# Both out projections of a two-layer encoder trunk by Strassen's algorithm on 12 of 16 K tiles

## The chip, the cores and the metric

The kernel runs on one core of a Trainium2 chip. The metric is device time in microseconds (us) of the whole program. A core has TensorE (PE in the profile: matmuls; PEld: the load of the stationary operand, here called the weight load), VectorE (DVE), ScalarE (ACT), GpSimd (POOL), and SyncE (SP), whose queue issues most transfers. Each engine works through its own queue in order; semaphores join them.

## The reference

The trunk has two layers over 512 tokens of width 2048, in float32. The change touches the last product of each layer, `concat([...]) @ w_out`, with a residual added:

```python
def even_layer(x, ...):
    proj = rmsnorm(x, ln_g) @ w_in
    ...
    return x + jnp.concatenate([na_o, dn_o, mem_o], axis=-1) @ w_out   # (512, 2048) @ (2048, 2048)

def odd_layer(x, ...):
    ...
    return x + jnp.concatenate([diff_o, mem_o], axis=-1) @ w_out       # (512, 2048) @ (2048, 2048)
```

Each branch (`na_o`, `dn_o`, `mem_o`, `diff_o`) is multiplied by its SiLU gate before the concatenation.

## The kernel before, in words

Activations lie transposed: 16 K tiles of 128 features (partitions) by 512 tokens. A float32 product is made as three matmuls on operands that are split into a high and a low part: high weight by high activation, high by low, low by high. ACT makes the high part (a rounding copy), DVE the low part (a subtraction). Tiles named `wr` are raw weights from DRAM, `wh` and `wl` their high and low parts, `hi` and `lo` those of activations, `w` (or `w2`) general work tiles of 128 by 512, `pa` the PSUM banks.

`WStream` holds all weights in the order of their use. Each time that PE's code takes a unit of weights, the stream emits the splits for the unit that is three ahead (`SPLIT_BUFS = 3` buffers each of `wh` and `wl`) and loads for raw tiles beyond that. PE's order is that in which the code is written. The orders on DVE, ACT, POOL and SP are made by a scheduler at build time and are fixed in the program: an instruction that waits holds up everything behind it on its engine.

`gates` ends a layer: for each of 16 tiles a product of 48 matmuls (`group`: 16 K tiles times 3, weights stationary, 512 token columns moving), then a SiLU on DVE and ACT, and a multiplication into the tile `mix[i]`. `out_proj` follows: for each of 16 output tiles `j` one `group` over the 16 K tiles, whose operands `mh[k]`, `ml[k]` are split from `mix[k]` by the hook `make` during the first. `consume` adds the residual, which comes by a transfer on SP's queue: `to_x1` (layer 0) also stores the sum to DRAM (`x1_d`), adds its squares to `acc1` and splits it into the operands `xh`, `xl` of layer 1; `to_out` (layer 1) stores the output. Gate weights and out-projection weights come in raw tiles of 128 by 1024 (eight K tiles of 128 columns). Long-lived operands have a pool of 34 tiles (`hl`, 17 pairs), work tiles another of 34 (`NW2`). Layer 0's branch outputs wait for their gates in DRAM (`mix_d`, `keep`); layer 1's stay in SBUF.

## Time and profile before

| what | value |
|---|---|
| median of 3 runs (lowest to highest) | 2024.88 us (2024.31 to 2026.25) |
| profiled execution, span from first to last instruction | 2021.8 us |
| PE busy | 2002.1 us, 99% of the span |
| DVE, ACT, POOL busy | 1155.9, 759.7, 129.8 us |
| mean granted TensorE clock | 0.998 of full speed |
| HBM traffic | 106 GB/s over the span |

No other time of the profiled execution is given than its span; the median of the runs is 3.1 us above it. Busy shares are means over stages. Where PE is busy throughout a stage, only its own instructions count there. A matmul's recorded duration covers its passage through the array, and the next one starts before it ends: what a matmul costs is read from the distance between two starts.

### The profile page before, as it was taken

What the parts mean: (1) busy time and instruction counts of PE and PEld (TensorE: products, weight loads), DVE (VectorE), ACT (ScalarE), POOL (GpSimd) and SP (SyncE); (2) the same over time, 40 slices, a digit from 0 to 9 for tenths busy, and PEclk for the clock granted to TensorE, in tenths of its full rate; (3) what the DMA queues carried; (4) which work ended last, traced back from release to release, by engine and by line L of the source; (5) the groups of instructions that cost most, each with busy time, mean ns of one, the idle gap of its engine ahead of it and who ended that gap; (6) DMA issues with size and microseconds to landing.
All of it is one profiled execution on the core that took longest, in us unless ns stands there. A gap on an engine that the chain in (4) does not pass through costs nothing.

```text
span 2021.8 us, 27331 instructions
## 1 busy us (share of the span) xinstructions
PE 2002.1 (99%) x10843; PEld 1741.7 (86%) x10843; DVE 1155.9 (57%) x2147; ACT 759.7 (38%) x1334; POOL 129.8 (6%) x124
## 2 busy tenths in 40 slices
PE   9999999999999999999999999999999999999999
PEld 7988899998988888888888889889899898888887
DVE  6676676767585766445334456566465656345222
ACT  5555344433343343324223343433434334223211
POOL 0100020201020202000000000100001000000000
PEclk9999999999999999999999999999999999999999
DMA  6454432222322233233444322122221222223332
GB/s 214 155 166 171 133 99 89 89 91 89 97 85 91 90 100 112 85 106 126 146 141 140 129 75 77 60 93 75 74 84 64 83 84 73 94 94 130 141 141 89
DMA packets 97503, 216.09 MB, mean 107 GB/s; under 512 B 21808, under 2 KB 36448, under 8 KB 97376
## 3 DMA queue, kind: packets, MB, share of 16 engines
q1 hardware_dynamic: 67776, 201.16, 29.1%
q10 hardware_dynamic: 29600, 13.19, 2.5%
q8 instruction: 85, 1.39, 0.3%
q14 instruction: 42, 0.34, 0.1%
HBM read 196.81 MB, written 17.51 MB: 106 GB/s over the span
## 4 chain that ended last, share of the span: by engine, by line
PE 96%; DVE 2%; DMA 1%; issue 1%; POOL 0%; ACT 0%; ACTq 0%; SPq 0%; DVEq 0%; POOLq 0%
PE pa L263 92%; PE pa L333 4%; DVE w L205 1%; DMA w<-in_xT_dram 0%; DMA w<-in_lvl_dram 0%; DVE s L205 0%; DMA w<-x_d 0%; POOL w L205 0%; DVE wl L205 0%; DVE vn L205 0%; POOL s L205 0%; DVE vb L205 0%; DVE S L205 0%; ACT wh L205 0%; ACT vd L205 0%
## 5 line engine op out<-in xcount | busy, mean ns | idle before, releaser
L205 ACT ACTIVATE wh<-wr 128x1024 fp32r<-128x1024 f32 (+3 forms) x333 | 341.7, 1027 | 720.5 <-PE pa L263 529.2
L205 DVE TENSOR_TENSOR wl<-wr,wh 128x1024 fp32r<-128x1024 f32 (+3 forms) x333 | 397.4, 1194 | 311.5 <-ACT wh L205 310.7
L263 PE MATMUL pa<-hi,wh 128*128 128x512 f32 x1312 | 518.1, 395 | 0.0
L263 PE MATMUL pa<-hi,wl 128*128 128x512 f32 x1312 | 511.6, 390 | 0.0
L263 PE MATMUL pa<-lo,wh 128*128 128x512 f32 x1312 | 511.3, 390 | 0.0
L263 PE MATMUL pa<-wh,hi 128*128 128x512 f32 (+3 forms) x1280 | 450.0, 352 | 2.4 <-ACT wh L205 2.4
L263 PE MATMUL pa<-wl,hi 128*128 128x512 f32 (+3 forms) x1280 | 439.5, 343 | 0.1
L263 PE MATMUL pa<-wh,lo 128*128 128x512 f32 (+3 forms) x1280 | 439.1, 343 | 0.0
L263 PEld LDWEIGHTS pa<-hi,wl 128*128 128x128 f32 x1312 | 246.4, 188 | 51.6
L263 PEld LDWEIGHTS pa<-hi,wh 128*128 128x128 f32 x1312 | 246.6, 188 | 49.1 <-DVE vb L205 0.5
L263 PEld LDWEIGHTS pa<-lo,wh 128*128 128x128 f32 x1312 | 246.7, 188 | 48.3
L263 PEld LDWEIGHTS pa<-wh,hi 128*128 128x128 f32 x1280 | 243.2, 190 | 23.2 <-ACT wh L205 3.2
L263 PEld LDWEIGHTS pa<-wh,lo 128*128 128x128 f32 x1280 | 242.8, 190 | 20.5
L263 PEld LDWEIGHTS pa<-wl,hi 128*128 128x128 f32 x1280 | 243.3, 190 | 19.2 <-DVE wl L205 0.6
L263 PE MATMUL pa<-w,w 128*128 128x256 f32 (+5 forms) x1416 | 191.9, 283 | 2.5 <-DVE w L205 1.6
L205 ACT ACTIVATE w<-pa 128x512 f32<-128x512 f32 (+4 forms) x234 | 123.2, 549 | 188.4 <-PE pa L333 134.6
L263 PEld LDWEIGHTS pa<-w,w 128*128 128x128 f32 (+2 forms) x1416 | 172.7, 181 | 17.1 <-issue 3.6
L205 DVE TENSOR_TENSOR w<-pa,w 128x512 fp32r<-128x512 f32 (+2 forms) x108 | 71.3, 679 | 147.9 <-PE pa L263 108.2
L205 POOL TENSOR_TENSOR s<-s,mhalf 128x1 f32<-128x1 f32 (+3 forms) x58 | 68.6, 1182 | 1190.8 <-DVE s L205 1187.8
L205 ACT ACTIVATE w<-w 128x512 f32<-128x512 f32 (+3 forms) x207 | 112.5, 578 | 55.1 <-DVE w L205 45.2
L205 ACT ACTIVATE w<-pa,s 128x256 f32<-128x256 f32 (+1 forms) x104 | 58.7, 570 | 128.8 <-DVE s L205 112.7
L333 PE MATMUL pa<-ct,w 128*128 128x128 f32 x712 | 100.4, 273 | 3.1 <-DMA w<-x_d 2.5
(148 smaller groups left out, 1461.0 us busy)
## 6 DMA issues: line engine op xcount, KB each, us to landing
wr<-in_wo_dram SPq DMA_DIRECT2D x112, 512.0 KB, 3.2
wr<-in_we_dram SPq DMA_DIRECT2D x75, 512.0 KB, 3.3
wr<-in_weo_dram SPq DMA_DIRECT2D x32, 512.0 KB, 3.2
wr<-in_woo_dram SPq DMA_DIRECT2D x32, 512.0 KB, 3.2
wr<-in_we_dram SPq DMA_DIRECT2D x40, 384.0 KB, 3.0
w<-in_xT_dram SPq DMA_DIRECT2D x32, 256.0 KB, 4.5
wr<-in_wek_dram SPq DMA_DIRECT2D x16, 512.0 KB, 4.1
wr<-in_wok_dram SPq DMA_DIRECT2D x16, 512.0 KB, 3.4
```

Source lines behind the costliest of these rows:

```text
L205: return f(*a, **k)
L263: nc.tensor.matmul(o, lhsT, rhs, start=start, stop=stop)
L333: nc.tensor.transpose(o, i, ident if idn is None else idn)
```

## The change

Both out projections are computed with the Winograd form of Strassen's algorithm on K tiles 0 to 11 and plainly on tiles 12 to 15. A unit `u` is 256 output columns (two output tiles). Six pairs of K tiles (0 and 1, 2 and 3, ...) form the two K halves; the two halves of the tokens (256 each) and the two halves of the unit's columns (128 each) are the other block indices. Seven block products of 6 K tiles replace eight. In `product`, an operand tile holds the high part in columns 0 to 255 and the low part in 256 to 511, so that the high weight takes one matmul of 512 columns, and the low weight one of 256; `fold` adds the two halves of the bank. The block sums of the activations are made once for each pair (`make_pair`: four sums on POOL, seven splits on ACT and DVE), those of the weights once for each unit (in `WStream.make`, kinds 5 and 7 on POOL, 6 and 4 on DVE), in place in the raw tiles. The sums of the products are added on ACT, POOL and DVE (`fold`, `unit`).

The plain part of a unit (`plain_part`, 24 matmuls of 512 columns, residual added) runs three units ahead of its products. Layer 0's results no longer become layer 1's operands at once: `to_x1` stores them, and `make_x1` reloads and splits them, three after output tile 11, three after 13, the rest later. The constants of layer 1 (`setup1`) are made after output tile 7. One pool of 62 tiles replaces the two of 34. Raw weight tiles hold up to 1536 columns, four of them. Layer 1's branch outputs are parked in DRAM too (`keep1`). The gates get a hook that makes the operands of the plain tiles after gate 6 and of pair 0 after gate 9.

```diff
-    def out_proj(mix, order, consume):
-        mh, ml = [None] * KT, [None] * KT
-
-        def make(i):
-            k = order[i]
-            mh[k], ml[k] = hl2()
-            split1(mh[k], ml[k], mix[k])
-
-        for j in range(KT):
-            consume(j, run(group(mh, ml, order, make if j == 0 else None)))
...
-    return 8 if n == 128 else 4 if n == 256 else 2
+    return 8 if n == 128 else 16 if n == 256 else 2
...
+NP = 6
+PAIR_A = [2 * i for i in range(NP)]
+PAIR_B = [2 * i + 1 for i in range(NP)]
+PLAIN = [k for k in [12, 13, 14, 15] + list(range(12)) if k not in PAIR_A + PAIR_B]
+NPL = len(PLAIN)
+UNITS = D // 256
+AHEAD = 3
...
+    def plan_out(self, run):
+        row = KT * 256
+        def rest(u):
+            src, o = run[u]
+            self.plain(src, o, row, 2 * NP * 256, row)
+        for u in range(AHEAD):
+            rest(u)
+        for u in range(UNITS):
+            src, o = run[u]
+            two = (self.load_of(src, o, row, 0, NP * 256), self.load_of(src, o, row, NP * 256, 2 * NP * 256))
+            self.ops += [(i, two) for i in PRODUCTS]
+            if u + AHEAD < UNITS:
+                rest(u + AHEAD)
...
+                a, b = (self.raw[i].rearrange("p (k n) -> p k n", k=NP) for i in ids)
+                r11, r12, r21, r22 = a[:, :, 0:128], a[:, :, 128:256], b[:, :, 0:128], b[:, :, 128:256]
+                if kind == 5:
+                    self.pool_e.tensor_tensor(r11, r12, r11, op=ALU.subtract)
+                elif kind == 6:
+                    self.vec.tensor_tensor(r11, r22, r11, op=ALU.subtract)
+                elif kind == 4:
+                    self.vec.tensor_tensor(r21, r21, r11, op=ALU.subtract)
+                elif kind == 7:
+                    self.pool_e.tensor_tensor(r12, r22, r12, op=ALU.subtract)
+                r = {1: r11, 5: r11, 6: r11, 2: r21, 4: r21, 3: r22, 7: r12}[kind]
+                hi, lo = self.hilo(NP * 128)
+                h3, l3 = (x.rearrange("p (k n) -> p k n", k=NP) for x in (hi, lo))
+                self.copy(h3, r)
+                self.vec.tensor_tensor(l3, r, h3.bitcast(F32), op=ALU.subtract)
+                if kind == PRODUCTS[-1]:
+                    for i in ids:
+                        del self.raw[i]
...
+PRODUCTS = (1, 5, 2, 6, 3, 4, 7)
+ORDER = {"eo": PAIR_A + PAIR_B + PLAIN, "oo": PAIR_A + PAIR_B + PLAIN}
+NW2 = 62
+RAW_BUFS = 4
...
+        def make_pair(p):
+            if p in sums:
+                return
+            a, b = mix[PAIR_A[p]], mix[PAIR_B[p]]
+            a11, a21, a12, a22 = a[:, 0:256], a[:, 256:512], b[:, 0:256], b[:, 256:512]
+            sa, sb = w2(), w2()
+            s1, s2, s3, s4 = sa[:, 0:256], sa[:, 256:512], sb[:, 0:256], sb[:, 256:512]
+            pool_e.tensor_tensor(s1, a21, a22, op=ALU.add)
+            pool_e.tensor_tensor(s2, s1, a11, op=ALU.subtract)
+            pool_e.tensor_tensor(s4, a12, s2, op=ALU.subtract)
+            pool_e.tensor_tensor(s3, a11, a21, op=ALU.subtract)
+            ops = {}
+            for i, src in ((1, a11), (2, a12), (4, a22), (5, s1), (6, s2), (3, s4), (7, s3)):
+                t = w2(F32R)
+                split1(t[:, 0:256], t[:, 256:512], src)
+                ops[i] = t
+            sums[p] = ops
+            mix[PAIR_A[p]] = mix[PAIR_B[p]] = None
...
+    def out_proj(ops, residual, consume):
+        plain, sums, make_plain, make_pair = ops
+        rest = {}
+        def plain_part(u):
+            xr = [w2(), w2()]
+            for j in range(2):
+                nc.sync.dma_start(xr[j], residual(2 * u + j))
+            hi, lo = W.op()
+            banks = [pb(), pb()]
+            for i in range(NPL):
+                xh, xl = plain[PLAIN[i]]
+                for j in range(2):
+                    c = slice(i * 256 + j * 128, i * 256 + (j + 1) * 128)
+                    mm(banks[j], hi[:, c], xh, start=(i == 0), stop=False)
+                    mm(banks[j], hi[:, c], xl, start=False, stop=False)
+                    mm(banks[j], lo[:, c], xh, start=False, stop=(i == NPL - 1))
+                    yield
+            for j in range(2):
+                vec.tensor_tensor(xr[j], banks[j], xr[j], op=ALU.add)
+            rest[u] = xr
+        def product(bank, i, first):
+            hi, lo = (x.rearrange("p (k n) -> p k n", k=NP) for x in W.op())
+            for p in range(NP):
+                x = sums[p][i]
+                mm(bank, hi[:, p, :], x, start=(first and p == 0), stop=False, more=not first)
+                mm(bank[:, 0:256], lo[:, p, :], x[:, 0:256], start=False, stop=(p == NP - 1), more=not first)
+                yield
+        def fold(o, bank, *more):
+            t = w2()[:, 0:256]
+            copy(t, bank[:, 256:512])
+            for m in more:
+                pool_e.tensor_tensor(t, t, m, op=ALU.add)
+            vec.tensor_tensor(o, bank[:, 0:256], t, op=ALU.add)
+        def unit(u):
+            f1, f2 = rest.pop(u)
+            c11, c21, c12, c22 = f1[:, 0:256], f1[:, 256:512], f2[:, 0:256], f2[:, 256:512]
+            s, t = w2(), w2()
+            p1, p5, u2, u3 = s[:, 0:256], s[:, 256:512], t[:, 0:256], t[:, 256:512]
+            a = pb()
+            yield from product(a, 1, True)
+            fold(p1, a)
+            b = pb()
+            yield from product(b, 5, True)
+            fold(p5, b)
+            pool_e.tensor_tensor(c22, c22, p5, op=ALU.add)
+            e = pb()
+            yield from product(e, 2, True)
+            fold(c11, e, p1, c11)
+            yield from product(a, 6, False)
+            fold(u2, a)
+            yield from product(b, 3, False)
+            fold(c12, b, u2, c12)
+            d = pb()
+            yield from product(d, 4, True)
+            fold(c21, d, c21)
+            yield from product(a, 7, False)
+            fold(u3, a)
+            pool_e.tensor_tensor(c21, c21, u3, op=ALU.add)
+            vec.tensor_tensor(c22, c22, u3, op=ALU.add)
+            consume(2 * u, f1)
+            consume(2 * u + 1, f2)
+        for k in PLAIN:
+            make_plain(k)
+        W.at += UNITS
+        for u in range(AHEAD):
+            run(plain_part(u))
+            for p in range(NP * u // AHEAD, NP * (u + 1) // AHEAD):
+                make_pair(p)
+        for u in range(UNITS):
+            run(unit(u))
+            if u + AHEAD < UNITS:
+                run(plain_part(u + AHEAD))
...
+        if j in (11, 13):
+            for _ in range(3):
+                make_x1()
+        if j >= 12:
+            kept[j] = f
...
+    out_proj(ops0, lambda j: xT[:, j, :], to_x1)
+    nlam, sub = setup
+    for k in range(len(xh), KT):
+        if k not in kept:
+            kept[k] = w2()
+            nc.sync.dma_start(kept[k], x1_d[:, k, :])
+    for _ in range(3):
+        make_x1()
...
+    mix1_d = dram.tile([P, KT, T], F32, name="mix1_d")
+    parked1 = {}
+    def keep1(i, f):
+        if i in (10, 11):
+            mix1[i] = f
+        else:
+            nc.sync.dma_start(mix1_d[:, i, :], f)
+            parked1[i] = mix1_d[:, i, :]
```

What this does to the fixed orders is shown at three places. The first is POOL's queue in layer 0's out projection. Before, nothing stands there: the last normalisation of the recurrent branch is followed by the first of layer 1 (`s` and `rstd1`, raised to the power of -0.5 by `mhalf`).

```order
L205 TENSOR_TENSOR s_8422<-s_8416,mhalf_80 128x4
L205 TENSOR_TENSOR s_8487<-s_8481,mhalf_80 128x4
L205 TENSOR_TENSOR rstd1_10417<-s_10419,mhalf_80 128x4
L205 TENSOR_TENSOR s_10447<-s_10444,mhalf_80 128x16
L205 TENSOR_TENSOR s_10977<-s_10974,mhalf_80 128x16
```

Now each unit has nine instructions there; these are unit 2's, where `w2_9085` and `w2_9084` are the unit's two results, `w2_9575` and `w2_9576` its running sums, and `wr_9491` and `wr_9666` the raw weights of unit 3.

```order
L282 TENSOR_TENSOR w2_9085<-w2_9085,w2_9575 128x256
L282 TENSOR_TENSOR w2_9636<-w2_9636,w2_9575 128x256
L282 TENSOR_TENSOR w2_9636<-w2_9636,w2_9084 128x256
L282 TENSOR_TENSOR w2_9682<-w2_9682,w2_9576 128x256
L282 TENSOR_TENSOR w2_9682<-w2_9682,w2_9085 128x256
L282 TENSOR_TENSOR w2_9706<-w2_9706,w2_9084 128x256
L282 TENSOR_TENSOR wr_9491<-wr_9491 128x6x128
L282 TENSOR_TENSOR wr_9491<-wr_9666,wr_9491 128x6x128
L282 TENSOR_TENSOR w2_9084<-w2_9084,w2_9576 128x256
```

The last addition into the unit's first result stands behind both weight sums of the next unit.

The second place is DVE's queue where the out projection of layer 0 begins, from the last gate's product (`rhB` is the tokens' scale) on. Before, the last operand's split (`lo_9033`) and the first output tile's residual addition (`w2_9041`) stand there among weight splits (`wl`), and `lo_9046` makes the first operand of layer 1.

```order
L205 TENSOR_TENSOR wl_8978<-wr_8823,wh_8977 128x1024
L205 TENSOR_TENSOR lo_9033<-w2_8524,hi_9032 128x512
L205 TENSOR_TENSOR w2_9041<-pa_8914,w2_9039 128x512
L205 TENSOR_TENSOR wl_9051<-wr_8853,wh_9050 128x1024
L205 SCALAR_TENSOR_TENSOR lo_9046<-w2_9041,vt_77,hi_9045 128x512
L205 TENSOR_TENSOR wl_9081<-wr_8919,wh_9080 128x1024
```

Now the splits of pairs 1 to 5 stand there, seven each; the first of them, and the residual additions of the first plain part (`w2_8929`, `w2_8930`):

```order
L282 TENSOR_TENSOR w2_8583<-w2_8583,w2_8921 128x512
L282 TENSOR_TENSOR w2_8973<-w2_7918,w2_8973 128x256
L282 TENSOR_TENSOR w2_8976<-w2_8008,w2_8976 128x256
L282 TENSOR_TENSOR w2_8979<-w2_8008,w2_8979 128x256
L282 TENSOR_TENSOR w2_8982<-w2_8967,w2_8982 128x256
L282 TENSOR_TENSOR w2_8985<-w2_8967,w2_8985 128x256
L282 TENSOR_TENSOR w2_8929<-pa_8939,w2_8929 128x512
L282 TENSOR_TENSOR w2_8930<-pa_8940,w2_8930 128x512
L282 TENSOR_TENSOR w2_8988<-w2_8968,w2_8988 128x256
L282 TENSOR_TENSOR w2_8991<-w2_8968,w2_8991 128x256
L282 TENSOR_TENSOR wl_8999<-wr_8828,wh_8998 128x768
```

Four further pairs of seven follow, with one more `wl` of 768 and four more residual additions between them, up to the first product's end: 35 splits of 256, two of 768 and six residual additions in all from the last gate on.

The third place is DVE's queue at the start of unit 6 of layer 0. Before, an output tile there has an addition of the residual, a weight split, the squares and another weight split.

```order
L205 TENSOR_TENSOR w2_9185<-pa_9122,w2_9183 128x512
L205 TENSOR_TENSOR wl_9197<-wr_9084,wh_9196 128x1024
L205 TENSOR_TENSOR acc1_8913<-acc1_8913,w2_9188 128x512
L205 TENSOR_TENSOR wl_9227<-wr_9127,wh_9226 128x1024
L205 TENSOR_TENSOR w2_9258<-pa_9195,w2_9256 128x512
```

Now three splits of reloaded tiles (`lo_10371`, `lo_10377`, `lo_10383`) stand ahead of the fold of the unit's first product (`w2_10386<-pa_10388`); `w2_9740` is the second result of unit 5.

```order
L282 TENSOR_TENSOR w2_9740<-w2_9740,w2_10206 128x256
L282 TENSOR_TENSOR wl_10411<-wr_10097,wh_10410 128x768
L282 TENSOR_TENSOR acc1_8928<-acc1_8928,w2_10361 128x512
L282 TENSOR_TENSOR wr_10121<-wr_10121,wr_10097 128x6x128
L282 TENSOR_TENSOR acc1_8928<-acc1_8928,w2_10365 128x512
L282 TENSOR_TENSOR wl_10432<-wr_10121,wh_10431 128x768
L282 TENSOR_TENSOR wl_10454<-wr_10121,wh_10453 128x768
L282 SCALAR_TENSOR_TENSOR lo_10371<-w2_10368,vt_74,hi_10370 128x512
L282 SCALAR_TENSOR_TENSOR lo_10377<-w2_10374,vt_74,hi_10376 128x512
L282 SCALAR_TENSOR_TENSOR lo_10383<-w2_10380,vt_74,hi_10382 128x512
L282 TENSOR_TENSOR w2_10386<-pa_10388,w2_10405 128x256
```

On SP's queue the reload of the third tile (`w2_10380`) stands behind a load of layer 1's weights into a raw tile (`wr_10477`) that comes free when `wl_10454` has been made:

```order
L1468 DMA x1_d_8927<-w2_9739 128x512
L1468 DMA x1_d_8927<-w2_9740 128x512
L1461 DMA w2_10368<-x1_d_8927 128x512
L1461 DMA w2_10374<-x1_d_8927 128x512
L162 DMA wr_10477<-in_wo_dram 128x1024
L1461 DMA w2_10380<-x1_d_8927 128x512
```

Unit 7 has the same sequence.

## Rows read from the trace of the kernel before

**Rows 1.** The page: busy time by engine; the chain that ended last, by engine.

```profile
PE 2002.1 (99%) x10843; PEld 1741.7 (86%) x10843; DVE 1155.9 (57%) x2147; ACT 759.7 (38%) x1334; POOL 129.8 (6%) x124
...
PE 96%; DVE 2%; DMA 1%; issue 1%; POOL 0%; ACT 0%; ACTq 0%; SPq 0%; DVEq 0%; POOLq 0%
```

**Rows 2.** Windows, out projections: length, PE, PEld, DVE, ACT, POOL busy; clock, DMA share, GB/s.

```profile
939.00:1114.00 175.00, 175.00 (x775) 145.00 (x774) 73.30 (x93) 52.58 (x66) 0.00 (x0) 1.00 0.43 142
1844.00:2018.00 174.00, 173.90 (x768) 143.71 (x766) 51.49 (x54) 32.80 (x32) 0.00 (x0) 1.00 0.36 128
```

**Rows 3.** Timeline of DVE, layer 0's out projection: start, duration, instruction, idle before.

```profile
993.74 0.69 DVE L205 TENSOR_TENSOR w<-pa,w 128x512 f32<-128x512 f32 x1 [3.30 <-PE pa L263]
...
1004.62 0.69 DVE L205 TENSOR_TENSOR w<-pa,w 128x512 f32<-128x512 f32 x1 [3.30 <-PE pa L263]
```

**Rows 4.** Timeline of PE, a chunk of layer 1 with 256 moving columns.

```profile
1212.82 0.28 PE L263 MATMUL pa<-wh,lo 128*128 128x256 f32 x1
1212.94 0.28 PE L263 MATMUL pa<-wh,hi 128*128 128x256 f32 x1
```

**Rows 5.** Groups by form: count, busy us, mean ns of one, idle before.

```profile
L205 DVE TENSOR_TENSOR wl<-wr,wh 128x1024 fp32r<-128x1024 f32 x283 | 348.4, 1232 | 284.0 <-ACT wh L205 283.3
...
L205 DVE TENSOR_TENSOR wl<-wr,wh 128x768 fp32r<-128x768 f32 x40 | 39.7, 992 | 19.0 <-ACT wh L205 18.9
...
L205 ACT ACTIVATE wh<-wr 128x768 fp32r<-128x768 f32 x40 | 33.7, 843 | 59.3 <-PE pa L263 43.9 <-issue 12.2 <-ACT w L205 1.7
...
L205 DVE SCALAR_TENSOR_TENSOR lo<-w,vt,hi 128x512 fp32r<-128x512 f32 x32 | 22.2, 746 | 2.6 <-ACT hi L205 2.6
L205 DVE TENSOR_TENSOR w<-pa,w 128x512 f32<-128x512 f32 x32 | 22.1, 691 | 108.2 <-PE pa L263 108.2
...
L205 ACT ACTIVATE hi<-w,vt 128x512 fp32r<-128x512 f32 x32 | 21.1, 711 | 4.8 <-DMA w<-in_xT_dram 4.8
...
L205 DVE TENSOR_TENSOR acc<-acc,w 128x512 f32<-128x512 f32 x30 | 20.6, 687 | 1.2 <-ACT w L205 0.5
...
L205 ACT ACTIVATE w<-pa 128x256 f32<-128x256 f32 x36 | 13.8, 384 | 16.3 <-PE pa L263 16.3
...
L205 DVE TENSOR_TENSOR macc<-macc,w 128x256 f32<-128x256 f32 x15 | 6.3, 419 | 0.0
```

**Rows 6.** Timeline of DVE, a recurrent head with POOL idle.

```profile
364.56 0.34 DVE L205 SCALAR_TENSOR_TENSOR w<-w,G,ct 128x128 f32<-128x128 f32 x1
```

**Rows 7.** Timeline of POOL in the last recurrent head, then of DVE there.

```profile
776.88 1.29 POOL L205 TENSOR_TENSOR w<-w,w 128x512 f32<-128x512 f32 x1 [2.78 <-ACT w L205]
779.06 5.44 POOL L205 TENSOR_TENSOR w<-w,w 128x512 f32<-128x512 f32 x2 [0.90 <-ACT w L205]
...
776.92 1.40 DVE L205 SCALAR_TENSOR_TENSOR w<-w,sG,ct 128x128 f32<-128x128 f32 x1
...
781.60 1.75 DVE L205 TENSOR_TENSOR wl<-wr,wh 128x1024 fp32r<-128x1024 f32 x1 [0.48 <-ACT wh L205]
```

**Rows 8.** Transfers of residuals, layer 0 (window 940:1110), then layer 1: issue to landing.

```profile
L1264 SPq DMA_DIRECT2D w<-in_xT_dram x16: 328/424/426, 942.2 to 1103.6; - x16
...
DMA to landing us min/median/max: 2.6/2.8/3.5
...
DMA to landing us min/median/max: 2.8/3.6/3.7
```

**Rows 9.** PE at the kernel's start: timeline, then windows (columns as in Rows 2).

```profile
8.13 0.79 PE L263 MATMUL pa<-wh,hi 128*128 128x512 f32 x1 [2.41 <-ACT wh L205]
...
11.30 0.63 PE L263 MATMUL pa<-wh,hi 128*128 128x512 f32 x1
11.73 0.63 PE L263 MATMUL pa<-wl,hi 128*128 128x512 f32 x1
...
10.00:15.00 5.00, 5.00 (x14) 3.96 (x13) 4.37 (x7) 5.00 (x9) 0.00 (x0) 0.54 1.04 391
15.00:20.00 5.00, 5.00 (x24) 4.14 (x23) 5.00 (x9) 5.00 (x9) 0.00 (x0) 1.00 1.06 391
```

More of the change, by code (lines that the diff above doesn't have):

```diff
@@ L77, in plan @@
     items += [("e", c) for c in E_GATE]
-    items += [("eo", _r(j * 128, 128)) for j in range(16)]
+    items += [("eo", _r(u * 256, 256)) for u in range(UNITS)]
     items.append(("o", _r(6144, 512)))
@@ L108, in pieces, with load @@
         return [slice(i * w // n, (i + 1) * w // n) for i in range(n)]
-    def load(self, upto):
-        while self.loaded < min(upto, len(self.todo)):
-            src, o, w = self.todo[self.loaded]
-            raw = self.pool.tile([P, w], F32, tag="wr", bufs=RAW_BUFS, name="wr")
-            dram = self.aps[src][o:o + P * w].rearrange("(p f) -> p f", p=P)
+    def load(self, upto=0):
+        while self.loaded < len(self.loads) and (len(self.raw) < RAW_BUFS or self.loaded < upto):
+            src, o, row, c0, c1 = self.loads[self.loaded]
+            w = c1 - c0
+            raw = self.pool.tile([P, NP * 256], F32, tag="wr", bufs=RAW_BUFS, name="wr")[:, 0:w]
+            dram = self.aps[src][o:o + P * row].rearrange("(p f) -> p f", p=P)[:, c0:c1]
             for c in self.pieces(self.loaded, w):
@@ L120, in load, with hilo @@
             self.loaded += 1
+    def hilo(self, w):
+        return (self.pool.tile([P, 1024], F32R, tag="wh", bufs=SPLIT_BUFS, name="wh")[:, 0:w],
+                self.pool.tile([P, 1024], F32R, tag="wl", bufs=SPLIT_BUFS, name="wl")[:, 0:w])
     def make(self, upto):
-        while self.made < min(upto, len(self.todo)):
-            w = self.todo[self.made][2]
-            self.load(self.made + 1)
-            raw = self.raw.pop(self.made)
-            hi = self.pool.tile([P, w], F32R, tag="wh", bufs=SPLIT_BUFS, name="wh")
-            lo = self.pool.tile([P, w], F32R, tag="wl", bufs=SPLIT_BUFS, name="wl")
-            for c in self.pieces(self.made, w):
-                self.copy(hi[:, c], raw[:, c])
-                if self.after and c.start == 0:
-                    self.after.pop(0)()
-                self.vec.tensor_tensor(lo[:, c], raw[:, c], hi[:, c].bitcast(F32), op=ALU.subtract)
+        while self.made < min(upto, len(self.ops)):
+            kind, ids = self.ops[self.made]
+            self.load(ids[-1] + 1)
+            if kind == 0:
+                raw = self.raw.pop(ids[0])
+                w = raw.shape[1]
+                hi, lo = self.hilo(w)
+                for c in self.pieces(self.made, w):
+                    self.copy(hi[:, c], raw[:, c])
+                    if self.after and c.start == 0:
+                        self.after.pop(0)()
+                    self.vec.tensor_tensor(lo[:, c], raw[:, c], hi[:, c].bitcast(F32), op=ALU.subtract)
+            else:
+                a, b = (self.raw[i].rearrange("p (k n) -> p k n", k=NP) for i in ids)
[16 more added lines that the diff above has]
+                        del self.raw[i]
@@ L138, in width, with op @@
         return len(self.items[self.at][1])
+    def op(self):
+        u = self.unit
+        self.unit += 1
+        self.make(u + SPLIT_BUFS)
+        self.load()
+        return self.ready.pop(u)
     def ks(self):
@@ L256, in tile_hybrid, with mm @@
     act = Timed(nc.scalar, clock, "act", 180.0, 0.83).activation
-    def mm(o, lhsT, rhs, start, stop):
+    def mm(o, lhsT, rhs, start, stop, more=False):
         n = 1
@@ L664, in mem_attention, with gates @@
             lanes.add(1, head(h))
-    def gates(xh, xl, rows, order, mix, parked=()):
-        for i in order:
+    def gates(xh, xl, rows, order, mix, parked=(), then=None):
+        for g, i in enumerate(order):
             if i in parked:
@@ L1267, in to_x1, with make_x1 @@
+    kept, setup = {}, []
+    def make_x1():
+        k = len(xh)
+        raw = kept.pop(k, None)
+        if raw is None:
+            raw = w2()
+            nc.sync.dma_start(raw, x1_d[:, k, :])
+        hi, lo = hl2()
+        split(hi, lo, raw, V("o_ln", k))
+        xh.append(hi)
+        xl.append(lo)
+    def to_x1(j, f):
         nc.sync.dma_start(x1_d[:, j, :], f)
         sumsq_add(acc1, f, j == 0)
-        hi, lo = hl2()
-        split(hi, lo, f, V("o_ln", j))
-        xh.append(hi)
@@ L1277, in tile_hybrid, with more_x1 @@
+    def more_x1(k):
+        while len(xh) <= min(k + 1, KT - 1):
+            make_x1()
     mix1 = [None] * KT
```

159 lines of the change are left out of this document (90 added, 69 removed).

## Prediction

> **What bounds the kernel now.** I read the page first, for the engine that ends last: PE is busy for 2002.1 us, 99% of the span, and holds 96% of the chain [rows 1]. Then the windows of the two stages that change: in both out projections PE is busy throughout at granted clock 1.00, while DVE works 42% and 30% of the time, ACT 30% and 19%, POOL not at all [rows 2]. So these stages cost what PE's own instructions cost, and the change must be judged by two things: how much PE work goes, and whether three engines that now have slack can feed what is left. The timeline of DVE gives PE's price: two residual additions, each at the end of 48 matmuls of 512 columns and each having waited for PE, start 10.88 us apart, so a matmul costs 10.88/48 = 0.2267 us [rows 3]. The timeline of PE has two matmuls of 256 columns 0.12 apart [rows 4]. The groups by form give the side engines' prices [rows 5].
>
> **PE.** Before: 2 layers x 16 tiles x 48 x 0.2267 = 348.2 us, which the two windows bear out. After, for each layer: 8 units x 24 plain matmuls x 0.2267 = 43.5, and 8 x 7 x 6 pairs of one 512 and one 256 x (0.2267 + 0.120) = 116.5; 160.0, twice 320.1. PE's work falls by **28.1 us**, if it is always fed. A unit is then 14.6 of products (2.08 each) and, where it has a plain part behind it, 5.4 more: 20.0.
>
> **Prices on the other engines.** On DVE a weight split of 768 is 0.99, one of 1024 1.23, an operand split of 256 as `macc` 0.42, of 512 0.69; a residual addition 0.69 [rows 5]. POOL has only additions of 512, 1.29 alone [rows 7]. For 256 the bounds are half of that and all of it (0.65 to 1.29); for 768, all and one and a half (1.29 to 1.94). DVE's rows leave a fixed part of 2 x 0.42 - 0.69 = 0.15; with the same in POOL I take 0.72 for 256 and 1.86 for 768.
>
> **DVE and POOL together.** Alone, DVE's 128x128 operation takes 0.34 [rows 6]. Beside POOL's addition it takes 1.40, starting at 776.92 and ending as POOL's ends; a weight split of 1.23 takes 1.75, and a pair of POOL additions 5.44 for 2 x 1.29 [rows 7]. So an operation of DVE with two SBUF inputs and one of POOL stand in line for each other, and I add their times. By the Trainium skill, SBUF — State Buffer, section "SBUF: two separate sides", the port pair that DVE and GpSimd share is an exclusive lock for such operations, held for the whole instruction, and an operation of DVE with only one SBUF input is outside it. The trace agrees with the first half by the 1.40; no row here shows the second, by which the head below would be 4.1 us a layer shorter. Speaking against this change is that it puts about nine POOL operations into each unit where none was.
>
> **The head of each out projection.** From the last gate on, DVE has its multiplication (0.7), 35 splits of 256 (14.7), two weight splits (2.0) and six residual additions (4.1): 21.5. PE has three plain parts of 24 matmuls and six matmul pairs of product 1, of which only the last part needs pair 5: 16.3 + 1.8 = 18.1 as cover. Without any sharing 3.4 are left over. In the same stretch POOL adds for pairs 3 to 5 (12 x 0.72) and twice for the next weights (2 x 1.86): 12.3. All in line: 33.8 - 18.1 = 15.7; if the PSUM readers overlap, 11.6. Products 5, 2 and 6 follow with splits that were queued behind. I take **16 per layer** (ends: 3.4, and with POOL at its upper prices 23).
>
> **Units 1 to 4, which have a plain part behind them.** A chain runs from the end of product 7: `u3` is folded, and POOL adds it to `c21`, but behind both weight sums of the next unit, as its queue shows (1.86 + 1.86 + 0.72). Only then does SP store the tile and issue the next two residuals, 0.42 each with the store, and these land 2.6 to 3.5 us after issue [rows 8]; then a residual addition and the weight split behind it on DVE (0.69 + 0.99). Together 4.44 + 1.26 + 2.8 + 1.68 = 10.2. PE's cover is the plain part and products 1 and 5, whose weights are split already: 5.4 + 4.2 = 9.6. The excess is 0.6; the second residual addition and the sum of kind 6 behind it add 0.69 and 0.99 before the next split, and where transfers land at 3.5 it is 0.7 more: 3.0 to 3.7 in all when they line up. I take **3.5** for units 1 to 3 of layer 0 and **7** for unit 4, where `setup1` puts some eight more DVE operations (of about 0.4) into the same queue. In layer 1 the landing is 3.6, but there are no squares: **2** each for four units. Ends: 0.5 and 7.
>
> **Units 5 to 7, with no plain part.** PE's unit is 14.6. DVE's operations with two SBUF inputs in layer 0: seven splits (6.94), two weight sums (1.98), an addition (0.42), two squares (1.37): 10.7, and seven additions and two sums on POOL (7 x 0.72 + 2 x 1.86 = 8.8): 19.5 in line, **4.9** over PE's. In layer 1 without the squares 18.1, **3.5** over. Ends: 0, if they overlap, and with POOL at 1.29 and 1.94 about 9.
>
> **The reloads of x1.** At the start of units 6 and 7 of layer 0 three splits of reloaded tiles stand in DVE's queue ahead of the fold of product 1, and the third reload stands on SP's queue behind a load that waits for `wl_10454`. From the end of the unit before, DVE first does 0.42 + 0.99 + 0.69 + 0.99 + 0.69 + 0.99 + 0.99 = 5.8; then SP's issue (0.42), a landing (2.8), ACT's rounding copy (0.71), DVE's split (0.75), ACT's copy out of PSUM (0.38) and the fold (0.42): 11.3. Product 6 adds into product 1's bank, so PE can run only products 1, 5 and 2 meanwhile, but the splits for 2 and 6 wait in the same queue: about 2 us of cover remains. **9.4** in each. Ends: 5, if product 5 covers too, and 11.3.
>
> **At nothing.** Parking layer 1's outputs adds transfers to a stage at a DMA share of 0.43 or less [rows 2], each a gate (10.9 us) ahead of its use. The late `make_x1` calls (ACT 0.71, DVE 0.75) lie beside 12 matmuls each (2.7 us); if that cover were gone, 10 x 0.75. Wider raw tiles carry the same bytes. The pool of 62 costs nothing unless a tile's release is late, which the chains above already hold.
>
> **The end and the clock.** Behind the last matmul come an ACT copy, a fold and a POOL addition (0.38 + 0.42 + 0.72) instead of one residual addition: **1**. After an idle 2.41 us at the start PE's matmuls are 0.43 apart, and the granted clock is 0.54 from 10 to 15 us, 1.00 from 15 on [rows 9]: the lower level, 1.2 GHz. That window holds 14 matmuls where the next holds 24, so a fall costs ten matmuls, 2.3 us, and 0.9 more in the stretch from 8.13 to 10: 3.2. The heads and the x1 reloads are long enough for it, four places, 12.8; where PE waits for DVE again soon after, the slower clock is hidden. I take **5**.
>
> **The sum.** Layer 0: 16 + 3 x 3.5 + 7 + 3 x 4.9 + 2 x 9.4 = 67.0. Layer 1: 16 + 4 x 2 + 3 x 3.5 = 34.5. With 1 and 5: 107.5 of new stalls against 28.1 saved: +79.4. The profiled span 2021.8 becomes 2101.2; the median of the runs is 3.1 above the span, which makes **2104**.
>
> **The rivals.**
>
> *The engines share less than I add up* (in line only where rows 7 shows it at its worst). Heads 3.4 plus pair 5's four additions (2.9), both layers 12.6; 1 in each of eight units with a plain part, 8; units 5 to 7 nothing; reloads 8 each, 16; end and clock 3. 39.6 - 28.1 = +11.5: **2036**. For it: DVE and ACT idle most of the stage today [rows 2]. Against it: 1.40 for 0.34.
>
> *The clock falls after every stall.* By the rows, 3.2 us for each of 16 units instead of 5 in all: +46, **2150**. For it: a wait of 2.41 us was followed by the lower level [rows 9]. Against: most waits I forecast are shorter than that. The Trainium skill, TensorE: Matmul & The Clock Gate, section "Part 1: The HAM clock gate", says the clock rests at half and sustained activity releases it; the start of this trace agrees with its 0.54, and no row here shows a fall in mid-program.
>
> *PE stays fed, and the kernel is faster.* One mechanism: POOL and DVE run side by side, and the residuals and reloads are issued early enough. It decides when all stalls together are below 28 us, 14 a layer. If only the heads (3.4 each) and the end are left, 2024.9 - 28.1 + 7.8 = **2005**. For it: DVE's own work is less than PE's in every unit. Against: queues are in order, and the chain through store, residual and split is 10.2 against 9.6 even with nothing shared.
>
> *No change within measurement*: the stalls equal 28 by accident. Some 0.2%, 4 us, is about what a measurement of this kernel can tell from no change.
>
> **How the numbers follow.** The forecast gets 0.62, less sharing 0.19, the clock 0.08, faster 0.07, no change 0.04. The forecast's own range, by the ends of its terms (heads 11.6 or 23, units 5 to 7 at 2 or 7), is 2070 to 2140. Reaching down to the less-sharing case at 2036 leaves about 2 in 10 outside: 2036 to 2142. Slower: 0.62 + 0.19 + 0.08 = 0.89.
>
> **What the profile after would show.** PE's busy time in out-projection windows without stalls is 160 a layer; each such stage should be 195 to 230 us long, layer 0's longer than layer 1's by some 30. Each head should have one idle stretch of PE of 10 to 16 us, ended by DVE (an operand split). POOL's group of 256 should have means above 0.72 and DVE's splits of 768 above 0.99, as they wait for each other. In units 6 and 7 of layer 0 DVE should wait for a DMA into a `w2` tile. The granted clock should be below 1 behind the heads and reloads. The prediction is wrong in its largest term if POOL's 256 takes under 0.65 beside DVE, or if the heads stall under 5 us; it is wrong in sign if PE's idle time in each stage is under 14 us.

## The result and the profile after

The changed kernel takes 2089.63 us (median of 4 runs, 2088.75 to 2091.78) against 2024.6 for the one before: ratio 1.0323, interval 1.0308 to 1.0337. It is slower by 65 us, as forecast; 2104 was 14 too many. The profiled execution's span went from 2021.8 to 2087.4.

The page after, busy time by engine and the chain that ended last (of before in [rows 1]):

```profile
PE 2000.0 (96%) x11035; PEld 1742.1 (83%) x11035; DVE 1333.9 (64%) x2431; ACT 849.7 (41%) x1570; POOL 354.7 (17%) x316
...
PE 80%; issue 6%; DVE 5%; POOL 5%; DMA 3%; ACT 1%; SPq 0%; POOLq 0%; DVEq 0%; ACTq 0%
```

PE's busy time is hardly less, although 24 us of matmuls went: layer 0's out projection is busy for 174 us, where PE's own work is 162, because matmuls at the lower clock take longer (granted clock 0.50 to 0.82 in the stretches below) and a stretch counts as busy while one is in the array. The chain says more: PE's share of it fell from 96% to 80%. The windows show where (columns as in [rows 2]): the head of layer 0, a steady unit of layer 0, its unit 6, then a steady unit of layer 1.

```profile
965.00:970.00 5.00, 1.05 (x7) 0.68 (x5) 3.93 (x6) 3.36 (x10) 4.92 (x6) 0.79 0.01 3
970.00:975.00 5.00, 1.26 (x3) 0.76 (x4) 5.00 (x11) 3.44 (x10) 2.92 (x4) 0.50 0.00 0
...
1025.00:1048.00 23.00, 20.89 (x110) 17.46 (x111) 16.86 (x23) 9.94 (x17) 11.00 (x9) 1.00 0.42 138
...
1113.00:1142.00 29.00, 17.68 (x87) 14.69 (x86) 15.84 (x23) 10.93 (x19) 10.50 (x9) 0.82 0.24 82
...
1970.00:1990.00 20.00, 20.00 (x109) 17.18 (x108) 15.66 (x21) 8.78 (x15) 11.01 (x9) 1.00 0.46 158
```

In the head PE has ten matmuls in 10 us, while POOL is full in the first five of them and DVE in the second. A steady unit (products and plain part) takes 23 us in layer 0 and 20 in layer 1, with the same nine POOL operations.

The unit lengths below are worked out from the starts of PE's matmuls (us, the seven products alone; a plain part behind one takes 5.45; a unit that PE never waits in takes 14.83; "start" is the first plain matmul, "u7" of layer 1 runs to the program's end, which comes 6.0 us after the last matmul in the changed kernel). In layer 1, e1 and e5 stay within 0.8 us of the changed kernel, and e9 and e10 within 0.5 of e8, over all eight units.

| kernel | layer | start | u0 | u1 | u2 | u3 | u4 | u5 | u6 | u7 |
|---|---|---|---|---|---|---|---|---|---|---|
| changed | 0 | 948.1 | 25.97 | 17.37 | 17.40 | 17.44 | 21.10 | 16.54 | 29.75 | 28.29 |
| | 1 | 1896.3 | 26.27 | 14.83 | 14.74 | 14.82 | 14.98 | 19.01 | 17.90 | 24.81 |
| e1 | 0 | 947.2 | 26.46 | 17.15 | 17.50 | 17.23 | 21.48 | 19.99 | 25.93 | 24.97 |
| e2 | 0 | 947.7 | 26.67 | 15.21 | 16.68 | 17.02 | 20.56 | 16.72 | 28.55 | 29.21 |
| | 1 | 1892.8 | 26.53 | 14.83 | 14.73 | 14.99 | 14.84 | 14.73 | 18.42 | 24.56 |
| e3 | 0 | 947.6 | 28.56 | 14.83 | 14.83 | 14.83 | 16.18 | 14.83 | 27.97 | 27.32 |
| | 1 | 1881.3 | 29.06 | 14.83 | 14.83 | 14.83 | 14.83 | 14.83 | 14.84 | 21.16 |
| e5 | 0 | 947.3 | 26.66 | 17.16 | 17.07 | 17.33 | 21.87 | 20.08 | 20.98 | 21.49 |
| e6 | 0 | 946.5 | 22.59 | 14.83 | 14.83 | 14.83 | 16.18 | 14.83 | 17.43 | 17.71 |
| | 1 | 1854.2 | 22.80 | 14.82 | 14.83 | 14.83 | 14.83 | 14.83 | 14.84 | 21.15 |
| e7 | 0 | 948.3 | 17.06 | 14.83 | 14.83 | 14.83 | 20.37 | 16.29 | 19.15 | 17.84 |
| | 1 | 1857.7 | 17.12 | 14.83 | 14.83 | 14.83 | 14.84 | 15.85 | 14.56 | 21.27 |
| e8 | 0 | 941.9 | 17.12 | 14.83 | 14.83 | 14.83 | 19.75 | 16.43 | 17.56 | 17.70 |
| | 1 | 1849.1 | 17.06 | 14.83 | 14.83 | 14.83 | 14.84 | 15.98 | 14.84 | 21.16 |
| e9 | 0 | 944.2 | 17.08 | 14.83 | 14.83 | 16.78 | 16.71 | 16.71 | 19.13 | 17.86 |
| e10 | 0 | 943.7 | 17.08 | 14.83 | 14.83 | 18.34 | 16.61 | 17.48 | 17.22 | 17.52 |

The two long units of layer 0 look like this in DVE's timeline, here unit 6 (idle before, and what ended it, in brackets):

```profile
1121.30 1.42 DVE L282 SCALAR_TENSOR_TENSOR lo<-w,vt,hi 128x512 fp32r<-128x512 f32 x2 [0.29 <-ACT hi L282]
1125.80 0.75 DVE L282 SCALAR_TENSOR_TENSOR lo<-w,vt,hi 128x512 fp32r<-128x512 f32 x1 [3.09 <-ACT hi L282]
1126.47 0.75 DVE L282 TENSOR_TENSOR w<-pa,w 128x256 f32<-128x256 f32 x2
```

and in ACT's and PE's:

```profile
1125.05 0.72 ACT L282 ACTIVATE hi<-w,vt 128x512 fp32r<-128x512 f32 x1 [3.16 <-DMA w<-x_d]
```

```profile
1126.94 0.79 PE L340 MATMUL pa<-w,wh 128*128 128x512 f32 x1 [9.29 <-DVE w L282]
```

The fold of product 1 (the first of the two at 1126.47) stands behind the third reloaded tile's split, which waits for ACT, which waits for the transfer; PE waits 9.29 us for that fold.

In layer 1 the order on SP's queue is another than the one the prediction reasons with. Behind units 0 to 3 both residuals of the plain part are issued ahead of the unit's stores; the first line below is from the end of unit 3, whose stores follow at 2006.50. Only behind unit 4 does a residual, the very last, stand behind a store, and DVE waits 3.01 us for it in unit 5 (SP's timeline, then DVE's):

```profile
1998.67 0.86 SPq L802 DMA_DIRECT2D w<-x_d  x2
...
2027.94 0.45 SPq L802 DMA_DIRECT2D w<-x_d  x1
...
2031.18 0.69 DVE L282 TENSOR_TENSOR w<-pa,w 128x512 f32<-128x512 f32 x1 [3.01 <-DMA w<-x_d]
```

Groups by form in layer 0's out projection, POOL then DVE (columns as in [rows 5]):

```profile
L282 POOL TENSOR_TENSOR w<-w,w 128x256 f32<-128x256 f32 x67 | 69.4, 1046 | 107.7 <-DVE w L282 75.3 <-ACT w L282 30.8 <-POOL w L282 0.2
L282 POOL TENSOR_TENSOR wr<-wr 128x768 f32<-128x768 f32 x16 | 32.2, 2013 | 14.5 <-DMA w<-in_xT_dram 9.5 <-DVE wl L282 4.5
```

```profile
L282 DVE TENSOR_TENSOR wl<-wr,wh 128x768 fp32r<-128x768 f32 x56 | 61.8, 1110 | 13.1 <-ACT wh L282 13.1
L282 DVE TENSOR_TENSOR w<-pa,w 128x256 f32<-128x256 f32 x56 | 22.8, 418 | 29.1 <-POOL w L282 28.4 <-ACT w L282 0.7
L282 DVE TENSOR_TENSOR w<-w,w 128x256 fp32r<-128x256 f32 x35 | 18.2, 577 | 1.3 <-ACT w L282 1.3
```

### The profile page after: what moved, and what is told of

Its sections match the earlier page's. It is cut to its first block, busy times and chain, and to the rows that moved or that the text cites. A ratio compares the mean times of both kernels' runs of the same rounds, so it can differ in the third digit from the quotient of the medians.

```text
span 2087.4 us, 28785 instructions
## 1 busy us (share of the span) xinstructions
PE 2000.0 (96%) x11035; PEld 1742.1 (83%) x11035; DVE 1333.9 (64%) x2431; ACT 849.7 (41%) x1570; POOL 354.7 (17%) x316
## 4 chain that ended last, share of the span: by engine, by line
PE 80%; issue 6%; DVE 5%; POOL 5%; DMA 3%; ACT 1%; SPq 0%; POOLq 0%; DVEq 0%; ACTq 0%
PE pa L340 76%; PE pa L409 4%; POOL w L282 3%; DVE w L282 2%; POOL wr L282 2%; DVE wl L282 2%; DMA w<-in_xT_dram 1%; DMA w<-x_d 1%; DVE wr L282 0%; ACT wh L282 0%; DMA w<-in_lvl_dram 0%; ACT w L282 0%; POOL s L282 0%; DMA wr<-in_weo_dram 0%; DVE s L282 0%
## 5 line engine op out<-in xcount | busy, mean ns | idle before, releaser
L340 PE MATMUL pa<-hi,wh 128*128 128x512 f32 x928 | 368.4, 397 | 0.0
L340 PE MATMUL pa<-hi,wl 128*128 128x512 f32 x928 | 361.9, 390 | 0.0
L340 PE MATMUL pa<-lo,wh 128*128 128x512 f32 x928 | 361.7, 390 | 0.0
L340 PE MATMUL pa<-w,wh 128*128 128x512 f32 x672 | 250.8, 413 | 37.3 <-DVE w L282 36.2
L282 POOL TENSOR_TENSOR w<-w,w 128x256 f32<-128x256 f32 (+1 forms) x184 | 203.5, 1117 | 382.5 <-DVE w L282 161.1
L282 ACT ACTIVATE w<-pa 128x256 f32<-128x256 f32 (+4 forms) x346 | 164.6, 492 | 231.6 <-PE pa L409 136.6
L340 PE MATMUL pa<-w,wl 128*128 128x256 f32 x672 | 195.5, 291 | 21.5 <-DVE wl L282 21.5
L340 PEld LDWEIGHTS pa<-hi,wl 128*128 128x128 f32 x928 | 174.2, 188 | 37.0
L340 PEld LDWEIGHTS pa<-hi,wh 128*128 128x128 f32 x928 | 174.4, 188 | 34.5 <-DVE vb L282 0.5
L340 PEld LDWEIGHTS pa<-w,wh 128*128 128x128 f32 x672 | 132.1, 197 | 73.5 <-DVE w L282 41.2
```

Of the source, the lines that this page charges most:

```text
L282: return f(*a, **k)
L340: nc.tensor.matmul(o, lhsT, rhs, start=start, stop=stop, skip_group_check=more)
```

## The experiments

The kernel before was timed again beside each group of runs: 2023.4 us (e1 to e4), 2025.6 (e5 to e8) and 2023.8 (e9 and e10). "Less" below is the difference of medians; across groups one or two us of it say nothing. By the ratios to the kernel before, e1 is 5.5 us under the changed kernel and e5 14.8.

**e1_reload_early.** The reloads of the first six operands of layer 1 are issued a unit ahead.

```diff
+        if j in (9, 11):
+            for k in range(3 * (j - 9) // 2, 3 * (j - 7) // 2):
+                kept[k] = w2()
+                nc.sync.dma_start(kept[k], x1_d[:, k, :])
         if j in (11, 13):
             for _ in range(3):
...
```

> The changed kernel, but the reloads of layer 1's first six operands are issued one unit ahead of their splits (three behind output tile 9, three behind 11); the splits stay in their places. Theory A (the two stalls of 9.57 and 9.55 us in units 6 and 7 of layer 0 are DVE waiting for the reload with the fold of product 1 queued behind it): both stalls nearly go; the last three units of layer 0, now 30.9 us over PE's own 43.7, come to about the 11.9 of layer 1 and 4 for their squares, so some 15 us less, 2075. Rival (the reload is only one of many late things, the splits and the copies on ACT and DVE take the same time in the queue): 5 us less or fewer, 2085.

2082.66 us, 7.0 less: between the two, nearer the rival. Units 6 and 7 lost 3.8 and 3.3 us; two waits of 5.7 us stayed where there had been two of 9.3. Unit 5 became 3.5 longer: the first three reloads (1.48 us of issuing) now stand ahead of the last two residuals on SP's queue, and DVE, which in the changed kernel waits 0.27 us for a residual there, waits 1.54 and makes its additions about 3 us later, with a fold behind them. In unit 6 DVE's timeline no longer shows a wait: it works without a gap from 1115.67 to the end of the fold at 1125.27, the splits still ahead of it.

```profile
1123.95 1.40 DVE L282 SCALAR_TENSOR_TENSOR lo<-w,vt,hi 128x512 fp32r<-128x512 f32 x2
1125.27 0.74 DVE L282 TENSOR_TENSOR w<-pa,w 128x256 f32<-128x256 f32 x2
```

So the transfer was somewhat over a third of that wait; e5 and e6 test what the rest was.

**e2_residuals_early.** `plain_part` gets its residual tiles, fetched ahead of the unit before it.

```diff
         for u in range(UNITS):
+            xr = residuals(u + AHEAD) if u + AHEAD < UNITS else None
             run(unit(u))
-            if u + AHEAD < UNITS:
-                run(plain_part(u + AHEAD))
+            if xr:
+                run(plain_part(u + AHEAD, xr))
```

> The changed kernel, but the residuals of a plain part are issued ahead of the unit that runs before it (two more tiles in use). Theory A (in units 1 to 3 of layer 0 the stall of 2.9 us each is the chain of store, residual, addition, split): 8.6 us less there and 1 to 3 in unit 4, together about 10, 2080. Rival (the weight sums on POOL and DVE ahead of the split set the time, and the residual is only the last of two things that end together): 2 us less or fewer, 2088.

2082.05 us, 7.6 less. Neither size came. In units 1 to 3 of layer 0 it took off 3.3 of 7.7 us, so the residual was one of two things that ended nearly together there, as the rival has it, though worth more than the rival's 2. Neither had the other 4.3: they came in unit 5 of layer 1, which fell from 19.01 to 14.73, PE's own, with POOL's work as it was. Its whole excess was the last residual behind its store.

**e3_no_pool.** The word `pool_e` becomes `vec` in the sums of `make_pair`, of kinds 5 and 7 and of `fold` and `unit`; for instance

```diff
-                    self.pool_e.tensor_tensor(r11, r12, r11, op=ALU.subtract)
+                    self.vec.tensor_tensor(r11, r12, r11, op=ALU.subtract)
...
-                pool_e.tensor_tensor(t, t, m, op=ALU.add)
+                vec.tensor_tensor(t, t, m, op=ALU.add)
```

> The changed kernel with all sums of the Strassen part that were on POOL (pairs, kinds 5 and 7, folds) on DVE. Theory A (DVE's operations with two SBUF inputs and POOL's stand in one line, so POOL adds no capacity and its 1.04 for 256 columns only lengthens the line against 0.42 on DVE): the last three units of layer 1 fall from 11.9 us over PE's work to about 8, the heads from 11.4 and 11.7 to about 10, chains through POOL shorten; some 8 us less, 2082. Rival (POOL works beside DVE for most of its time, and DVE gets about 5 us more work in every unit of 15 to 20): the units with a plain part stall in both layers, 5 to 20 us more, 2095 to 2110.

2064.41 us, 25 less: three times what theory A had, and the rival is out. DVE took all of POOL's work, and every unit with or without a plain part came to PE's own 14.83 but for unit 4 (16.18), the two reload units and the very last one; the heads became 2.6 and 2.8 us longer. DVE's own operations became shorter (layer 0, same window of stage):

```profile
L282 DVE TENSOR_TENSOR wl<-wr,wh 128x768 fp32r<-128x768 f32 x56 | 52.9, 950 | 12.8 <-ACT wh L282 12.8
...
L282 DVE TENSOR_TENSOR w<-pa,w 128x256 f32<-128x256 f32 x54 | 21.7, 416 | 1.1 <-ACT w L282 0.9
L282 DVE TENSOR_TENSOR w<-w,w 128x256 fp32r<-128x256 f32 x35 | 12.2, 414 | 0.0
```

The splits of 768 fell from 1.110 to 0.950 and those of 256 from 0.577 to 0.414, while the folds, which read PSUM and one tile, stood at 0.418 beside POOL and 0.416 without it. That is the rule of the Trainium skill, SBUF — State Buffer, section "SBUF: two separate sides", in both halves: operations with two SBUF inputs wait for POOL, those with one don't. That the folds did run beside POOL can be seen in the changed kernel's trace: of layer 0's 56 folds 20 overlap with an operation of POOL, and none of these takes more than 0.43; of the 56 splits of 768, the 24 that overlap take 1.33 on average and the others 0.95. Over the program POOL gave up 224 us of busy time and DVE's rose by 33 only. The folds' waits for POOL's sums (28.4 us) went too. So e3 takes away two things at once, POOL's slower additions in the chain and the waits that they put on DVE; how much of the 25 us each was worth it does not show.

**e4_pool_of_68.** The kernel before, with the shared pool alone.

```diff
-NW2 = 34
+NW2 = 68
...
-        return hl.tile([P, 512], F32R, tag="hi", name="hi"), hl.tile([P, 512], F32R, tag="lo", name="lo")
+        return (wk.tile([P, 512], F32R, tag="w2", name="hi"), wk.tile([P, 512], F32R, tag="w2", name="lo"))
```

> The kernel before with one part of the change alone: operands and work tiles share one pool (of 68 tiles, the same memory as the two of 34). Theory A (the 8.9 us that the changed kernel loses before its first out projection come from the orders that the shared pool brings, beginning with ACT's first operand copy, which stands behind four weight copies): the first product starts some 4 us later and the whole is 4 to 9 us longer than before, 2029 to 2034. Rival (they come from the four larger raw tiles and the loads that go out at once): no change, 2025.

2047.5 us, ratio to before 1.012 (1.0104 to 1.0135): 24 us slower, far beyond theory A. Up to the first out projection (939.0 in the kernel before) it lost 8.0 us; the changed kernel lost 9.1. The first product starts at 14.28 where before it was 8.13 [rows 9]: ACT's first operand copy stands behind four weight copies.

```profile
13.52 3.77 ACT L205 ACTIVATE hi<-w,vt 128x512 fp32r<-128x512 f32 x6
```

At the head of its first out projection ACT makes eleven operand copies in a row (5.82 us from 946.39) only when the gates have ended, and 7 us more are lost there; 4 more in layer 1. This part is e4's own, since the changed kernel makes other operands there.

**e5_splits_spread.** As e1, with the splits behind folds in the middle of units 6 and 7.

```diff
-        if j in (11, 13):
-            for _ in range(3):
-                make_x1()
...
             fold(c11, e, p1, c11)
+            mid(u)
...
             fold(c12, b, u2, c12)
+            mid(u)
...
             fold(c21, d, c21)
+            mid(u)
...
-    out_proj(ops0, lambda j: xT[:, j, :], to_x1)
+    out_proj(ops0, lambda j: xT[:, j, :], to_x1, lambda u: make_x1() if u >= 6 else None)
```

> The changed kernel; the reloads are issued one unit ahead as in e1_reload_early, and of the six splits of layer 1's operands one stands behind each fold of products 2, 3 and 4 of units 6 and 7 of layer 0, so that none stands ahead of the fold of product 1. e1 left two stalls of 6.0 us in which DVE was busy all the time with splits ahead of that fold. Theory A (half of the stall was the transfer, the other half the place of the splits in DVE's queue): units 6 and 7 fall from 29.8 and 28.3 us (25.9 and 25.0 in e1) to about 18 each, some 20 us less than the changed kernel, 2069. Rival (DVE's and POOL's line as a whole is too long for these units, wherever the splits stand): no better than e1, 2082.

2077.33 us, 12.3 less than the changed kernel and 5.3 less than e1: units 6 and 7 at 21 and 21.5, down from 29.8 and 28.3, while unit 5 stays as long as in e1. The place of the splits counted, and the rival is out as stated; but the units did not get to 18 until POOL's sums were gone from them as well (e6: 17.4 and 17.7).

**e6_units_on_dve.** As e5, and e3's edit but for `make_pair`, whose sums stay on POOL.

> As e5_splits_spread, and the weight sums of kinds 5 and 7 and the additions of the folds on DVE; the sums of the pairs stay on POOL. Theory A (in the units POOL's work in line with DVE's sets the time; in the head, where DVE is short of time, POOL helps): the units as in e3_no_pool without a stall (14.8 each with nothing behind), units 6 and 7 of layer 0 at 15 to 16, the heads back from 13.7 and 14.2 us to about 11 each: 2064 - 6 - 24 = 2034. Rival (the six splits need room on DVE that is no longer there once POOL's sums are on it): units 6 and 7 at 20, 2044.

2033.64 us, where theory A had 2034. That the number is so near is luck: against e3 the heads gave 12.2 us where 6 were expected, and units 6 and 7 gave 20.2 where 24 were. The heads fell to 7.8 and 8.0 over PE's own, perhaps since the sums of kinds 5 and 7 no longer stand between those of the pairs on POOL, which no run tests alone; units 6 and 7 stayed at 17.5.

**e7_five_ahead.** `AHEAD = 5` on e6.

> As e6_units_on_dve, with five plain parts (AHEAD = 5) ahead of the first unit instead of three, so units 3 and 4 have none behind them. Theory A (a head's stall of 11 us is what DVE and POOL need for the pairs over PE's cover, and two plain parts of 5.45 more cover it): both heads fall to about 1, the units without a plain part cost PE's own time, 20 us less than e6: 2014, under the kernel before. Rival (the cover is only moved: the units that lose their plain part stall by as much): as e6, 2034.

2028.78 us, 4.9 less than e6 instead of 20. (The two profiled executions, which the table shows, are only 1.3 us apart.) Both heads are down to 2.3, nearly the 1 that A has, and layer 1 keeps the gain. In layer 0, units 4 to 7 gave 7.5 back, as the rival has it. The windows say why (units 4 to 7 of layer 0, then most of layer 1's stage): over its units 4 to 7, with squares, constants and reloads, layer 0 keeps DVE busy for 17.4 us a unit, more than PE's 14.83, so that DVE sets the time; in layer 1's units 3 to 6 it is 14.1, and PE stays fed but for 1 us in unit 5.

```profile
1055.00:1127.00 72.00, 63.56 (x329) 52.47 (x328) 67.94 (x124) 38.12 (x68) 0.00 (x0) 0.95 0.39 130
1925.00:2020.00 95.00, 93.63 (x518) 80.31 (x518) 88.44 (x153) 47.31 (x81) 0.00 (x0) 1.00 0.36 120
```

**e8_first_operands.** On e7, `load_x(0)` and `load_x(1)` are called behind the first two fetches of x, and the loads of weights are held to what is asked for there.

```diff
     for i in range(3):
-        W.load(i + 1)
+        W.load(i + 1, False)
         if i > 0:
             fetch_x()
             fetch_x()
+        else:
+            load_x(0)
+            load_x(1)
```

> As e7_five_ahead, and the first two operands of the program are split ahead of the fetches of the other 14 tokens' tiles, with the weights' loads not all issued at once, so that ACT's first two operand copies stand first again. Theory A (of the 8.9 us lost before the first out projection, 4.3 come from the place of these copies behind four weight copies, since tiles of the shared pool are handed out in the program's order): first product at about 8 us again instead of 12.4, 4 us less than e7, 2010. Rival (PE waits there for the transfers, whatever the order): as e7, 2014.

2023.18 us, 5.6 less than e7 (4 expected). ACT's first operand copy starts at 7.07 and PE's first product at 8.36. The edit changes the place of the copies and that of the loads together; the run does not say which of the two counted.

Against the kernel before the ratio is 0.9985 (0.9976 to 0.9995): 0.15% under it, the only version here whose interval ends below 1. That is 2.4 us between the medians, about as much as the kernel before differs from one group of runs to another.

**e9_setup_early** and **e10_splits_three_units.** The constants of layer 1 after tile 5; then also two splits in each of units 5 to 7.

```diff
-        if j == 7:
+        if j == 5:
...
-        if j in (9, 11):
-            for k in range(3 * (j - 9) // 2, 3 * (j - 7) // 2):
+        if j in (7, 9, 11):
+            for k in (j - 7, j - 6):
...
-    out_proj(ops0, lambda j: xT[:, j, :], to_x1, lambda u: make_x1() if u >= 6 else None)
+    out_proj(ops0, lambda j: xT[:, j, :], to_x1, lambda u: make_x1() if u >= 5 else None)
```

> As e8_first_operands, with the constants of layer 1 made after output tile 5 instead of 7, in a unit that still has a plain part behind it. In e8, unit 4 of layer 0 takes 19.75 us where its neighbours take 14.83 and 16.43. Theory A (its 4.9 us are DVE's eight further operations and the table reads in a unit with no cover): 3 to 5 us less than e8, 2019. Rival (unit 4 stalls because it is the second unit without a plain part, and DVE is short of time there anyway): as e8, 2023.

> As e9_setup_early, with the six splits of layer 1's operands over units 5 to 7 of layer 0, two each, instead of three each in units 6 and 7 (17.56 and 17.70 us in e8). Theory A (a split more or less of 0.75 us in a unit with no plain part is a stall of that size): each of the two units 0.8 less, unit 5 up to 1.5 more, so within 1 us of e9. Rival (a unit has room for two splits and not for three): 3 us less than e9, 2016.

2024.99 us (1.0005, 0.9996 to 1.0014) and 2023.21 us (0.9996, 0.9988 to 1.0005): neither differs from before. In e9 unit 4 fell from 19.75 to 16.71, as A had it, but units 3 and 6 rose by 2.0 and 1.6 (unit 6 to what it was in e7), so that nothing was gained, as the rival had it. e10's median lies 1.8 us under e9's, between its theory A and its rival, but units 3 to 7 together take 87.2 us in both (e8: 86.3). With DVE full, work that is moved within these units stays on the path.

## Why the prediction was right, step by step

The sign and its reason hold: PE's work fell, and PE is not fed. Layer 0's stage takes 217.8 us, within the 195 to 230 that were forecast for each; layer 1's takes 185.0 up to its last matmul, which is under them. Term by term, from the table (over 14.83 a unit) and the spans:

| term | forecast | measured |
|---|---|---|
| PE's work | -28.1 | -24.0 (two stages of 162.2 in place of 174.2) |
| heads | 32 | 11.1 + 11.4 |
| units 1 to 3, then 4, of layer 0 | 10.5 + 7 | 7.7 + 6.3 |
| units 1 to 4 of layer 1 | 8 | 0.1 |
| units 5 to 7 of layer 0, reloads with them | 33.5 | 30.1 |
| units 5 to 7 of layer 1 | 10.5 | 11.0 |
| end, and the clock apart | 1 + 5 | 2.0, the clock being in the rows above |
| before the first out projection | 0 | 9.1 |

The measured terms make 64.8 of the span's 65.6. That the total is only 14 us off is in part luck: terms that were forecast too long come to some 28 us, and 13 of them are offset by the 9.1 that the forecast did not have at all and the 4.1 that it saved too much on PE.

- **PE's work.** A pair of matmuls takes 14.83 / 42 = 0.353 where PE is fed, not 0.347. (Behind a wait, products of 2.08 us are common, which is 0.347; why the pairs differ stays open.)
- **The heads** were the mis-sized term. The step that all stand in line was wrong for the PSUM readers (e3), and the forecast named that end, 11.6. The other part is DVE's price: seven splits of 256 behind each other take 2.42 us in e3, 0.345 from start to start, where I took the recorded 0.42; on PE I had read the distance of two starts and on DVE not. 35 splits are 2.6 us less for it.

```profile
976.79 2.42 DVE L282 TENSOR_TENSOR w<-w,w 128x256 fp32r<-128x256 f32 x7
```

With both, 15.7 becomes 9.0. Of the 2.1 to 2.4 that were measured above it, 1.2 is product 5, which runs at the lower clock in part (3.33 us for 2.08, granted clock 0.68 from 975 to 980); the rest is not accounted for. e6 and e7 show the head's mechanism: less POOL work in line, or more cover, and most of the stall goes.
- **POOL's prices** were right: alone, three additions of 256 take 2.10 at 1127.02, and one of 768, which starts with DVE idle, takes 1.82 at 1109.70 (0.72 and 1.86 forecast). The means over the stage, waits for DVE included, are 1.05 and 2.01.

```profile
1127.02 2.10 POOL L282 TENSOR_TENSOR w<-w,w 128x256 f32<-128x256 f32 x3 [10.98 <-ACT w L282]
```

- **The steady units.** In layer 0, 2.6 each for 3.5; but the chain through store and residual is less than half of it (e2), and with POOL's sums off the way nothing is left (e3). In layer 1 the step that failed is the order on SP's queue: the forecast takes the residuals to be issued behind the stores there too, and those that units 1 to 4 need are issued nearly 8 us ahead of them (1998.67 and 2006.50), so that 0.1 was left of the 8. Where one does stand behind a store, before unit 5, the chain costs 4.2, and e2 removes it.
- **Units 5 to 7 and the reloads.** The sizes hold in units 6 and 7: 14.9 and 13.5 over PE's own in layer 0 for 14.3 (9.29 of it a wait for 9.4), 3.1 and about 4 in layer 1 for 3.5. Of the reload's path e1 and e5 bear out both halves, transfer and place in the queue. That POOL's sums are the cause in layer 1's units 6 and 7 is shown by e3, which brings unit 6 to 14.84 and takes 2.8 off unit 7 up to the last matmul. Unit 5 does not fit: 1.7 in layer 0 for 4.9, and layer 1's 4.2 for 3.5 is the last residual and not the line (e2), so that the good total of layer 1's row is luck.
- **At nothing** was wrong in one place: the shared pool. e4 shows 8.0 us before the first out projection from it alone, e8 brings its start from 948.3 (e7) to 941.9 by the order in which the program takes its tiles and issues its first loads. Where the last 2.9 come from stays open, and so does why the scheduler lets the copies wait.
- **The clock.** The granted clock fell behind the head (0.50) and in unit 6 (0.82), as forecast, and nowhere in layer 1's steady units. It also fell in unit 4 of layer 0 (0.93 from 1071 to 1096) and unit 5 of layer 1 (0.91 from 2030 to 2048), which the forecast did not name.
- **The rivals.** Less sharing (2036) is out by the heads and e3. Lower clock everywhere is out: a steady unit of layer 0 waits and stays at 1.00. "PE stays fed" did come true in layer 1's units 1 to 4 alone, then in most units of e3 and in nearly all of e6 to e8; with stalls below the saving, as in e8, the kernel is level with the one before.
